# The start of an SSD-and-pooling decoder step on one core: another order of loads, weight splits and adaLN blocks

## The chip, the core and the metric

The kernel runs on one core of a Trainium2 chip. Its engines are PE (matrix products into PSUM), DVE (elementwise), ACT (functions and scaled copies), POOL (elementwise, slower) and SP, which here only issues transfers. Each engine works through its own queue in order; semaphores hold an instruction back until what it needs is there. The metric is the device time in microseconds (us), the median over executions.

## What is computed

A decoder trunk of two layers, on a prompt of 1024 positions and eight short sequences of eight positions (64), so 1088 columns in all. Each layer normalizes x, modulates it by an adaLN vector made from the conditioning c, mixes it and adds it back:

```python
sc = jax.nn.silu(c.astype(jnp.float32))
for i in range(DEPTH):
    mod = sc @ ada_w[i] + ada_b[i]
    shift, scale, gate = jnp.split(mod, 3, axis=-1)
    hn = rmsnorm(x, norm_g[i]) * (1.0 + scale[:, None]) + shift[:, None]
    if i % N_MIXERS == 0:
        out, cv, st = ssd_branch(hn, ...)      # starts with  zxbcdt = h @ w_in
    else:
        out, ps = pool_branch(hn, ...)
    x = x + (1.0 + gate[:, None]) * out
y = rmsnorm(x, final_norm_g)
```

Only the first lines of layer 0 matter here: the sum of squares of x, the adaLN shift and scale, hn, and the first products with w_in.

## The kernel before

x lies transposed: eight tiles of 128 features by 1088 columns (`xs[0..7]`). All 1088 columns are cut into three pieces for PSUM, `CH`, of 368, 368 and 352. To keep fp32 accuracy a matrix is split into a rounded part and the rest (for a weight `hi` on ACT by a copy, `lo` by a subtraction; for activations the tiles named hh and hl), and one product is three matmuls: hi by hh, hi by hl, lo by hh (`mm1`, L190 to L192).

`setup` issues the first loads, computes silu(c) into `scp`, and lets PE run 62 filler products (`warm`). `front` is the stage of this case:

- the squares of the eight x tiles on ACT (L1391, L1395), summed on DVE into `rst` (L1396), the last tile in the three pieces of CH;
- for each piece a matmul with ones that sums over the partitions (L302), logarithm and exponential on ACT (L305, L318), which leave 1/rms in `rst`;
- the adaLN blocks `ada_first(kt)`, kt from 0 to 7, one for each x tile: two halves of 512 KB from `adaA`, eight small matmuls (L261) into the PSUM tile am, a copy on ACT into mp (L266), two selecting matmuls with a 9-column part of the constants kc (L270, "sel" in what follows), and two DVE instructions that leave shift and scale (L280, L281);
- product steps k from 0 to 7. Step k modulates x tile k (`modulate`, L325 to L342: DVE, then ACT for hh, DVE for hl) and multiplies it by slice k of the first two weights, 18 matmuls of 3 pieces each into six PSUM tiles (named mm and p), and then by the small weight wdt (tile pdt, L1431). Step 0 is modulated in three pieces, the others whole.

The first two weights are split whole (`stream_split`, L141 and L145). After step 7 come products with whole streamed weights (tiles wh and wl).

The kernel is written with a tile framework that orders instructions by its own plan; `issue_after(ins)` makes what is inside come behind an instruction in that plan. So the order that counts is that of the built queues.

Of the kernel before, what the change touches and what calls it, by code (L numbers as in the profile page):

```python
# [8 lines left out]
F32 = mybir.dt.float32  # L9
# [35 lines left out]
LAST_USE = {4: 0, 7: 1}  # L45
NSLOT_A = 30
NSLOT_B = 7
NSLOT_E = 4
# [51 lines left out]
class Build:  # L100
# [87 lines left out]
    def mm1(self, ps, w, k, act, ch, first, last):  # L188
        nc, (hi, lo), (ah, al), (a, n) = self.nc, w, act, ch
        nc.tensor.matmul(ps[:, :n], hi[:, k, :], ah[:, a:a + n], start=first, stop=False)  # L190
        nc.tensor.matmul(ps[:, :n], hi[:, k, :], al[:, a:a + n], start=False, stop=False)  # L191
        nc.tensor.matmul(ps[:, :n], lo[:, k, :], ah[:, a:a + n], start=False, stop=last)  # L192

# [8 lines left out]
    def setup(self):  # L202
        nc, io, cp = self.nc, self.io, self.cp
        ct = self.tp.tile([P, 8, 9], F32, tag="ct", name="ct")
        nc.sync.dma_start(ct, io["cT"])
        self.xs = []
        for k in range(8):
            t = self.slots.get("x")
            nc.sync.dma_start(t, io["xT"][k])
            self.xs.append(t)  # L210
        self.vec = cp.tile([P, V_N], F32, tag="vec", name="vec")
        nc.sync.dma_start(self.vec, io["vec"])
        self.kc = cp.tile([P, K_N], F32, tag="kc", name="kc")
        nc.sync.dma_start(self.kc, io["kc"])
        self.ident = self.kc[:, K_ID:K_ID + 128]
# [30 lines left out]


    def ada_block(self, src):

        nc = self.nc  # L250
        raws = []
        for hh in range(2):
            if src is None:
                raws.append(self.stream_next_raw().rearrange("p a m -> p (a m)"))
            else:
# [10 lines left out]
        nc.scalar.activation(mp, pm[:, :256], AF.Copy)  # L266
        yield
        p2 = pm[:, 256:]
        for i in range(2):
            ins = nc.tensor.matmul(p2[:, 16 * i:16 * i + 9], mp[:, 128 * i:128 * i + 128], self.kc[:, K_SEL9:K_SEL9 + 9], start=True, stop=True)  # L270
        self.sel = ins.ins
        yield p2
# [47 lines left out]
    def modulate(self, l, k, x, rst, hi, lo, a, n, t):  # L320
# [13 lines left out]
        if pn < n:  # L334
# [5 lines left out]
            eng.tensor_tensor(out=ts, in0=ts, in1=self.shf[l][:, k, 0:8].unsqueeze(2).to_broadcast([P, 8, 8]), op=ALU.add)  # L340
            nc.scalar.activation(hi[:, s], t[:, pn:n], AF.Copy)
            last = eng.tensor_tensor(out=lo[:, s], in0=t[:, pn:n], in1=hi[:, s].bitcast(F32), op=ALU.subtract)  # L342
# [1039 lines left out]
    def front(self):  # L1382

        nc, io, sl = self.nc, self.io, self.slots
        xs = self.xs
        wdts = sl.get("wdt")
        wdt = wdts[:, :256].rearrange("p (k m) -> p k m", k=8)
        nc.sync.dma_start(wdt, io["wdt"])
        rst = sl.get("rst")
        with self.ln_set():  # L1390
            nc.scalar.activation(rst, xs[0], AF.Square)  # L1391
            for k in range(1, 8):
                sq = self.raw_tile()
                for a, n in CH if k == 7 else ((0, TOK),):
                    nc.scalar.activation(sq[:, a:a + n], xs[k][:, a:a + n], AF.Square)  # L1395
                    nc.vector.tensor_tensor(out=rst[:, a:a + n], in0=rst[:, a:a + n], in1=sq[:, a:a + n], op=ALU.add)  # L1396
# [6 lines left out]
        self.wslots = []  # L1403
# [4 lines left out]
        ws = [self.wsplit.pop(i) for i in range(2)]  # L1408
        self.wpos = 2
        pst = [[self.mm_tile() for _ in range(3)],  # L1410
               [self.pp.tile([P, 512], F32, tag=t, bufs=b, name=self.name("p0")) for t, b in (("y", 2), ("y", 2), ("S", 1))]]
# [513 lines left out]
```

## Time and profile before

| | |
|---|---|
| median of three runs | 1596.21 us (1596.17 to 1596.92) |
| the profiled execution | 1598.18 us |
| its span, first to last instruction | 1596.4 us |
| granted clock of TensorE over the span | 0.997 |
| first product of step 0 | 24.20 us after the span's start |
| first product with a wh tile, behind the eight steps | 67.39 us |

Timeline rows read: start and length in us, engine, line, operation, tile written and tiles read, shapes, number of instructions merged into the row, and in brackets the idle time ahead of it and what ended it. Matmul ends are modelled, so starts are the safer numbers. In the rows a weight load (PEld) is separate from the product (PE).

### The profile page before, as it was taken

Reading aid. Unit: us, or ns where it says so; the run is one execution under the profiler, and the core shown is the slowest. Engines: PE = TensorE matmul, PEld = TensorE weight load, DVE = VectorE, ACT = ScalarE, POOL = GpSimd, SP = SyncE. Lnnn points to the kernel's source line nnn. Section 1 sums busy time; section 2 is a strip of 40 time slices with the busy share of each in tenths; the row PEclk is TensorE's granted clock in tenths of the full one; section 3 lists DMA queues with packets and bytes.
Section 4 is the critical chain, followed back from the end, with each engine's and each line's share of the span. In section 5 each row is a group of like instructions: output and inputs, shape, how many; then the busy total and the mean of one; then the engine's idle time right before and its main releaser. Section 6 shows DMA issues by size and latency. Waiting matters only on the chain.

```text
span 1596.4 us, 30712 instructions
## 1 busy us (share of the span) xinstructions
PE 1573.5 (99%) x11946; PEld 1506.6 (94%) x11946; DVE 1299.4 (81%) x2152; ACT 790.1 (49%) x1512; POOL 519.4 (33%) x558
## 2 busy tenths in 40 slices
PE   8999999999999999999999999999999999999997
PEld 7899999998898998989998999999999999999997
DVE  6874879787888988899888868998889777667886
ACT  6663344466666666674555437533332233233364
POOL 0133556512322413141111232375666630000241
PEclk9999999999999999999999999999999999999999
DMA  9423232355555554679899532233333279566783
GB/s 354 166 101 107 73 112 83 107 185 168 174 161 168 177 195 131 228 245 317 300 336 315 190 128 73 70 133 102 116 113 110 104 246 371 137 180 178 164 170 118
DMA packets 122306, 275.59 MB, mean 173 GB/s; under 512 B 18192, under 2 KB 59312, under 8 KB 122160
## 3 DMA queue, kind: packets, MB, share of 16 engines
q1 hardware_dynamic: 118128, 260.90, 48.0%
q0 software_dynamic: 4032, 12.72, 4.7%
q8 instruction: 94, 1.54, 0.4%
q14 instruction: 52, 0.43, 0.1%
HBM read 201.12 MB, written 70.23 MB: 170 GB/s over the span
## 4 chain that ended last, share of the span: by engine, by line
PE 79%; DVE 8%; issue 4%; DMA 4%; ACT 4%; POOL 1%; SPq 0%; DVEq 0%; ACTq 0%; POOLq 0%
PE st L1061 10%; PE st L1059 10%; PE st L1060 10%; PE mm L190 10%; PE mm L191 9%; PE mm L192 9%; PE op L1278 2%; PE op L1279 2%; PE op L1277 2%; DMA acb<-acd 2%; PE S L616 2%; PE y L638 2%; DVE raw L368 1%; PE tr L577 1%; DVE xbc L359 1%
## 5 line engine op out<-in xcount | busy, mean ns | idle before, releaser
L1059 PE MATMUL st<-hh,w 128*128 128x272 f32 x832 | 240.5, 289 | 0.9 <-ACT w L182 0.9
L1061 PE MATMUL st<-hh,w 128*128 128x272 f32 x832 | 240.7, 289 | 0.4 <-DVE w L184 0.4
L1060 PE MATMUL st<-hl,w 128*128 128x272 f32 x832 | 240.3, 289 | 0.0
L1059 PE MATMUL st<-t,w 128*128 128x272 f32 x624 | 179.8, 288 | 0.0
L1061 PE MATMUL st<-t,w 128*128 128x272 f32 x624 | 179.7, 288 | 0.0
L1060 PE MATMUL st<-t,w 128*128 128x272 f32 x624 | 179.4, 287 | 0.0
L190 PE MATMUL mm<-hh,wh 128*128 128x368 f32 (+1 forms) x528 | 178.3, 338 | 0.0
L191 PE MATMUL mm<-hl,wh 128*128 128x368 f32 (+1 forms) x528 | 174.7, 331 | 0.0
L192 PE MATMUL mm<-hh,wl 128*128 128x368 f32 (+1 forms) x528 | 173.2, 328 | 0.0
L1059 PEld LDWEIGHTS st<-hh,w 128*128 128x128 f32 x832 | 156.9, 189 | 1.3 <-ACT w L182 1.3
L1061 PEld LDWEIGHTS st<-hh,w 128*128 128x128 f32 x832 | 156.6, 188 | 0.9 <-DVE w L184 0.9
L1060 PEld LDWEIGHTS st<-hl,w 128*128 128x128 f32 x832 | 156.9, 189 | 0.0
L182 ACT ACTIVATE w<-wr 128x512 fp32r<-128x512 f32 x104 | 64.9, 629 | 166.4 <-PE st L1061 137.4
L624 POOL TENSOR_TENSOR hd<-h,cd 128x256 f32<-128x256 f32 x56 | 47.2, 842 | 293.5 <-DVE h L625 146.5
L1278 PE MATMUL op<-b,w 128*128 128x272 f32 x448 | 129.2, 288 | 0.7 <-DVE b L1207 0.7
L1277 PE MATMUL op<-b,w 128*128 128x272 f32 x448 | 129.6, 289 | 0.0
L1279 PE MATMUL op<-b,w 128*128 128x272 f32 x448 | 129.1, 288 | 0.0
L190 PE MATMUL mm<-gh,wh 128*128 128x368 f32 (+1 forms) x372 | 125.6, 339 | 0.0
L192 PE MATMUL mm<-gh,wl 128*128 128x368 f32 (+1 forms) x372 | 122.2, 328 | 0.0
L191 PE MATMUL mm<-gl,wh 128*128 128x368 f32 (+1 forms) x372 | 122.0, 328 | 0.2 <-DVE gl L791 0.2
L1059 PEld LDWEIGHTS st<-t,w 128*128 128x128 f32 x624 | 117.8, 189 | 0.1
L1061 PEld LDWEIGHTS st<-t,w 128*128 128x128 f32 x624 | 117.5, 188 | 0.0
(310 smaller groups left out, 4593.8 us busy)
## 6 DMA issues: line engine op xcount, KB each, us to landing
wr<-win SPq DMA_DIRECT2D x48, 512.0 KB, 3.6
wr<-pin SPq DMA_DIRECT2D x32, 512.0 KB, 3.6
acb<-acd SPq DMA_DIRECT2D x62, 256.0 KB, 4.1
wr<-pout SPq DMA_DIRECT2D x28, 512.0 KB, 5.0
x<-x1d SPq DMA_DIRECT2D x24, 544.0 KB, 6.7
x1d<-x SPq DMA_DIRECT2D x22, 544.0 KB, 4.6
wr<-pout POOLq DMA_DIRECT2D x20, 512.0 KB, 5.7
x<-xT SPq DMA_DIRECT2D x16, 544.0 KB, 6.6
```

The lines of the kernel that those rows point to most:

```text
L182: self.nc.scalar.activation(hi, src, AF.Copy)
L190: nc.tensor.matmul(ps[:, :n], hi[:, k, :], ah[:, a:a + n], start=first, stop=False)
L191: nc.tensor.matmul(ps[:, :n], hi[:, k, :], al[:, a:a + n], start=False, stop=False)
L192: nc.tensor.matmul(ps[:, :n], lo[:, k, :], ah[:, a:a + n], start=False, stop=last)
L616: nc.tensor.matmul(S[:, 256 * i:256 * i + 256], Bt, xde.rearrange("p r q -> p (r q)"), start=True, stop=True)
L624: nc.gpsimd.tensor_tensor(out=hd, in0=h[-1], in1=cd.unsqueeze(2).to_broadcast([P, 4, 64]), op=ALU.mult)
L1059: nc.tensor.matmul(ps[c][:, :QUART], hi[:, k], xh[:, t], start=(k == 0), stop=False)
L1060: nc.tensor.matmul(ps[c][:, :QUART], hi[:, k], xl[:, t], start=False, stop=False)
L1061: nc.tensor.matmul(ps[c][:, :QUART], lo[:, k], xh[:, t], start=False, stop=(k == 3))
L1277: nc.tensor.matmul(ps[:, :QUART], hi[:, k], xh, start=k == 0, stop=False)
L1278: nc.tensor.matmul(ps[:, :QUART], hi[:, k], xl, start=False, stop=False)
L1279: nc.tensor.matmul(ps[:, :QUART], lo[:, k], xh, start=False, stop=k == 7)
```

## The change

Five things are different.

1. **Loads.** vec, the nine sel columns of kc (with one more), the first two of eight slices of the first two weights (`WK`), and the first half of adaLN block 0 go ahead of the x tiles. The second half of block 0 and the other six slices of both weights follow x. wdt and the rest of kc are issued from inside step 0.
2. **Splits.** The two weights are split in two parts each: slices 0 and 1 early (ACT and POOL), slices 2 to 7 behind the modulation of steps 0 and 1 (ACT and DVE).
3. **Squares.** The last two x tiles are squared and added by pieces, not the last alone.
4. **Block 0** is computed among the sums over the partitions instead of behind them.
5. **Blocks 1 to 3** have fixed places: behind the products (k, weight, piece) of `FIRST`; blocks 4 to 7 behind the last product of the steps before.

Slots of the same size are used as before, and nothing behind the front is edited. The diff, cut to its core:

```diff
+WK = 2
+FIRST = {(0, 0, 1): 1, (1, 0, 0): 2, (1, 1, 2): 3}
...
-        nc.tensor.matmul(ps[:, :n], lo[:, k, :], ah[:, a:a + n], start=False, stop=last)
+        return nc.tensor.matmul(ps[:, :n], lo[:, k, :], ah[:, a:a + n], start=False, stop=last)
...
-        self.xs = []
-        for k in range(8):
-            t = self.slots.get("x")
-            nc.sync.dma_start(t, io["xT"][k])
-            self.xs.append(t)
         self.vec = cp.tile([P, V_N], F32, tag="vec", name="vec")
         nc.sync.dma_start(self.vec, io["vec"])
         self.kc = cp.tile([P, K_N], F32, tag="kc", name="kc")
-        nc.sync.dma_start(self.kc, io["kc"])
+        nc.sync.dma_start(self.kc[:, K_SEL9:K_SEL64], io["kc"][:, K_SEL9:K_SEL64])
+        raws = [self.wp.tile([P, 8, P], F32, tag="wr", bufs=3, name=self.name("wr")) for _ in range(2)]
+        for i, t in enumerate(raws):
+            nc.sync.dma_start(t[:, :WK], self.items[i][0][:, :WK])
+        self.ada0 = [self.slots.get("ada") for _ in range(2)]
+        self.xs = [self.slots.get("x") for _ in range(8)]
+        self.load_ada(self.ada0[0], 0, 0)
+        for k in range(8):
+            nc.sync.dma_start(self.xs[k], io["xT"][k])
+        self.load_ada(self.ada0[1], 0, 1)
+        for i, t in enumerate(raws):
+            nc.sync.dma_start(t[:, WK:], self.items[i][0][:, WK:])
+        self.firsts = [self.split_first(t) for t in raws]
...
+        def part(a, b, eng):
+            self.nc.scalar.activation(hi[:, a:b], raw[:, a:b], AF.Copy)
+            eng.tensor_tensor(out=lo[:, a:b], in0=raw[:, a:b], in1=hi[:, a:b].bitcast(F32), op=ALU.subtract)
...
-        wdts = sl.get("wdt")
-        wdt = wdts[:, :256].rearrange("p (k m) -> p k m", k=8)
-        nc.sync.dma_start(wdt, io["wdt"])
         rst = sl.get("rst")
+        for _, _, part in self.firsts:
+            part(0, WK, nc.gpsimd)
...
-                for a, n in CH if k == 7 else ((0, TOK),):
+                for a, n in CH if k > 5 else ((0, TOK),):
...
+            self.ada_first(0)
             for a, n in CH:
                 self.ms_log(rst, rst, a, n, 1.0 / 1024, "mm", 3)
                 self.rstd(rst[:, a:a + n])
-        self.ada_first(0)
...
-        lower = [self.stream_split(i, True) for i in range(2)]
         with self.tc.issue_after(self.sel):
             self.warm(8, "mm", 3)
-        self.ada_first(1)
...
+        lower = [functools.partial(f[2], WK, 8, nc.vector) for f in self.firsts]
...
         for k in range(8):
-            if k < 6:
-                self.ada_first(k + 2)
+            if 1 < k < 6:
+                with self.tc.issue_after(mm.ins):
+                    self.ada_first(k + 2)
...
-                if lower:
+            if lower:
+                with self.tc.issue_after(last.ins), self.tc.issue_after(self.mod_hi.ins):
                     lower.pop(0)()
...
-                    self.mm1(pst[i][c], ws[i], k, (hi, lo), CH[c], k == 0, k == 7)
+                    mm = self.mm1(pst[i][c], ws[i], k, (hi, lo), CH[c], k == 0, k == 7)
+                    if (k, i, c) in FIRST:
+                        with self.tc.issue_after(mm.ins):
+                            self.ada_first(FIRST[k, i, c])
+                if k + i == 0:
+                    nc.sync.dma_start(wdt, io["wdt"])
+                    for a, b in ((0, K_SEL9), (K_SEL64, K_N)):
+                        nc.sync.dma_start(self.kc[:, a:b], io["kc"][:, a:b])
```

The built queues show where this puts things. SP's queue at the start of the program, before, from the last x tile on (the seven others and ct stand ahead; ada_324 and ada_326 are block 0, ada_362 begins block 1):

```order
L209 DMA x_191<-xT 128x1088
L212 DMA vec<-vec 128x282
L214 DMA kc<-kc 128x778
L1388 DMA wdt_282<-wdt 128x256
L257 DMA ada_324<-adaA 128x1024
L257 DMA ada_326<-adaA 128x1024
L121 DMA wr_343<-win 128x1024
L121 DMA wr_348<-win 128x1024
L257 DMA ada_362<-adaA 128x1024
```

The same queue now, from its first transfer to the first x tile (wr_181 and wr_182 are the two weights, ada_185 the first half of block 0):

```order
L207 DMA ct<-cT 128x72
L209 DMA vec<-vec 128x282
L211 DMA kc<-kc 128x10
L214 DMA wr_181<-win 128x256
L214 DMA wr_182<-win 128x256
L269 DMA ada_185<-adaA 128x1024
L219 DMA x_187<-xT 128x1088
```

So five transfers moved ahead of x; behind the eight x tiles stand ada_186, the two remaining weight parts (128x768), both halves of block 1, then wdt and kc.

PE's queue between the 62 fillers and the first product (mm_381), before; ms_320 is the third and last of the sums over the partitions:

```order
L302 MATMUL ms_320<-rst_284,ones 128x352
L261 MATMUL am_328<-ada_324,scp 32x256 x4
L261 MATMUL am_328<-ada_326,scp 32x256 x4
L270 MATMUL am_328<-kc,mp_337 128x9 x2
L245 MATMUL warm_353<-ones 128x128 x8
L190 MATMUL mm_381<-hh_407,w_13_345 128x368
```

The same place now, with all three sums (ms_347, ms_351, ms_355):

```order
L286 MATMUL am_332<-ada_185,scp 32x256 x4
L327 MATMUL ms_347<-rst_296,ones 128x368
L286 MATMUL am_332<-ada_186,scp 32x256 x4
L327 MATMUL ms_351<-rst_296,ones 128x368
L295 MATMUL am_332<-kc,mp_341 128x9 x2
L327 MATMUL ms_355<-rst_296,ones 128x352
L254 MATMUL warm_359<-ones 128x128 x8
L192 MATMUL mm_369<-hh_376,w_11_207 128x368
```

Block 0 moved in among the sums, and the third sum now stands between sel and the eight fillers.

ACT's queue from the end of block 0 to hh of step 1, before (hh_407 is step 0's, hh_469 step 1's; mp_375 belongs to block 1, w_13 and w_15 are the two weights):

```order
L266 ACTIVATE mp_337<-am_328 128x256
L141 ACTIVATE w_13_345<-wr_343 128x1024
L331 ACTIVATE hh_407<-x_177,shf_274 128x368 x2
L141 ACTIVATE w_15_350<-wr_348 128x1024
L333 ACTIVATE x_177<-x_177,shf_274 128x368 x2
L331 ACTIVATE hh_407<-x_177,shf_274 128x288
L341 ACTIVATE hh_407<-x_177 128x64
L266 ACTIVATE mp_375<-am_366 128x256
L333 ACTIVATE x_177<-x_177,shf_274 128x288
L331 ACTIVATE hh_469<-x_179,shf_274 128x1024
```

And now, from the second piece of step 0 on (hh_376 is step 0's, hh_441 step 1's, mp_416 belongs to block 1):

```order
L356 ACTIVATE hh_376<-x_187,shf_288 128x368
L358 ACTIVATE x_187<-x_187,shf_288 128x368
L356 ACTIVATE hh_376<-x_187,shf_288 128x288
L358 ACTIVATE x_187<-x_187,shf_288 128x368
L358 ACTIVATE x_187<-x_187,shf_288 128x288
L366 ACTIVATE hh_376<-x_187 128x64
L263 ACTIVATE w_11_207<-wr_181 128x768
L291 ACTIVATE mp_416<-am_407 128x256
L356 ACTIVATE hh_441<-x_188,shf_288 128x1024
```

The weight split moved behind all pieces of step 0, ahead of block 1's copy; the second weight's now stands behind hh of step 1. On PE block 1 stands whole between products of step 0, with 17 of its 18 products ahead of its sel; blocks 2, 4 and 7 stand between products of steps 1, 2 and 5, and blocks 3, 5 and 6 next to pdt. Before, blocks 1 and 2 were worked ahead of step 1's products, block 3 between products of step 1, and blocks 4 to 7 behind pdt. Behind step 7 the queues hold the same instructions, some DVE, ACT and SP rows up to the second pair of products in another order.

More of the change, by code (lines that the diff above doesn't have):

```diff
@@ L245, in warm, with split_first, load_ada @@
             self.nc.tensor.matmul(ps[:, :128], self.ones, self.ones, start=True, stop=True)
+    def split_first(self, raw):
+        hl = [self.slots.get("w0", F32R) for _ in range(2)]
+        hi, lo = (t[:, :1024].rearrange("p (k m) -> p k m", k=8) for t in hl)
+        def part(a, b, eng):
+            self.nc.scalar.activation(hi[:, a:b], raw[:, a:b], AF.Copy)
+            eng.tensor_tensor(out=lo[:, a:b], in0=raw[:, a:b], in1=hi[:, a:b].bitcast(F32), op=ALU.subtract)
+        return hl, (hi, lo), part
+    def load_ada(self, t, kt, hh):
+        self.nc.sync.dma_start(t[:, :1024].rearrange("p (a b) -> p a b", a=4), self.io["adaA"][0, kt][:, 4 * hh:4 * hh + 4, :])
     def ada_block(self, src):
@@ L1399, in front @@
                 self.rstd(rst[:, a:a + n])
[L1400 removed]
         self.hn = []
[L1403 to L1404 removed]
         with self.tc.issue_after(self.sel):
             self.warm(8, "mm", 3)
[L1407 to L1408 removed]
         self.wpos = 2
+        wdts = sl.get("wdt")
+        wdt = wdts[:, :256].rearrange("p (k m) -> p k m", k=8)
+        ws = [f[1] for f in self.firsts]
+        self.wslots = [t for f in self.firsts for t in f[0]]
+        lower = [functools.partial(f[2], WK, 8, nc.vector) for f in self.firsts]
         pst = [[self.mm_tile() for _ in range(3)],
```

4 lines of the change are left out of this document (3 added, 1 removed).

## The prediction

> **What bounds the kernel now.** I read the page first, then the busy time by stretches, then the timeline of the first 68 us engine by engine, because the diff touches nothing later than that.
>
> ```profile
> span 1596.4 us, 30712 instructions
> PE 1573.5 (99%) x11946; PEld 1506.6 (94%) x11946; DVE 1299.4 (81%) x2152; ACT 790.1 (49%) x1512; POOL 519.4 (33%) x558
> 24.20:33.04 8.84, 7.71 (x63) 4.36 (x62) 6.65 (x15) 5.22 (x10) 0.00 (x0) 1.00 1.01 405
> 67.39:116.00 48.61, 48.61 (x343) 48.61 (x343) 40.25 (x70) 32.57 (x56) 10.90 (x10) 1.00 0.27 99
> ```
>
> The columns of the last two rows are stretch, length, then busy time of PE, weight load, DVE, ACT and POOL, granted clock, DMA share, GB/s. PE is the bound of the whole; behind 67.39 it is full, so whatever the front wins or loses there goes through to the end. Only before 33.04 does PE stand and wait. What it waits for is the chain from the last x tile to the first product:
>
> ```profile
> 6.69 1.11 ACT L1395 ACTIVATE raw<-x 128x1088 f32<-128x1088 f32 x1 [0.26 <-DMA x<-xT]
> 14.90 1.30 ACT L1395 ACTIVATE raw<-x 128x368 f32<-128x368 f32 x3 [0.26 <-DMA x<-xT]
> 16.69 0.24 DVE L231 TENSOR_SCALAR cwh<-vec 128x160 f32<-128x160 f32 x1 [0.58 <-DMA vec<-vec]
> 16.95 1.42 DVE L1396 TENSOR_TENSOR rst<-rst,raw 128x368 f32<-128x368 f32 x3
> 17.54 2.10 PE L302 MATMUL ms<-rst,ones 128*128 128x368 f32 x6 [0.94 <-DVE rst L1396]
> 18.46 0.57 ACT L305 ACTIVATE rst<-ms,eps 128x368 f32<-128x368 f32 x1 [1.56 <-PE ms L302]
> 19.06 0.51 ACT L318 ACTIVATE rst<-rst 128x368 f32<-128x368 f32 x1
> 19.48 0.99 ACT L305 ACTIVATE rst<-ms,eps 128x368 f32<-128x368 f32 x2
> 21.28 1.17 DVE L338 TENSOR_TENSOR x<-x,rst 128x64 f32<-128x64 f32 x8 [2.56 <-ACT rst L318]
> 21.30 0.38 ACT L266 ACTIVATE mp<-am 128x256 f32<-128x256 f32 x1
> 21.73 0.61 PE L270 MATMUL am<-kc,mp 128*128 128x9 f32 x4 [0.50 <-ACT mp L266]
> 22.20 2.03 PE L245 MATMUL warm<-ones 128*128 128x128 f32 x16
> 22.45 0.23 DVE L280 TENSOR_SCALAR shf<-am,vec 128x9 f32<-128x9 f32 x1
> 22.91 1.11 DVE L325 SCALAR_TENSOR_TENSOR x<-x,scl,rst 128x368 f32<-128x368 f32 x2
> 23.55 1.12 ACT L331 ACTIVATE hh<-x,shf 128x368 fp32r<-128x368 f32 x2 [0.64 <-DVE x L325]
> 24.20 0.95 PE L190 MATMUL mm<-hh,w 128*128 128x368 f32 x2
> ```
>
> The last x tile is squared from 14.90; the additions of its pieces wait on DVE behind two instructions that need vec; all three pieces go through logarithm and exponential before adaLN block 0 is copied (21.30); the first product starts at 24.20. Next is the way to product step 1:
>
> ```profile
> 23.94 1.22 DVE L145 TENSOR_TENSOR w<-wr,w 128x1024 fp32r<-128x1024 f32 x1
> 24.57 1.04 ACT L141 ACTIVATE w<-wr 128x1024 fp32r<-128x1024 f32 x1
> 30.52 1.28 DVE L325 SCALAR_TENSOR_TENSOR x<-x,scl,rst 128x1024 f32<-128x1024 f32 x1
> 31.84 1.15 ACT L331 ACTIVATE hh<-x,shf 128x1024 fp32r<-128x1024 f32 x1 [2.13 <-DVE x L325]
> 33.04 0.60 PE L190 MATMUL mm<-hh,w 128*128 128x368 f32 x2 [0.48 <-ACT hh L331]
> ```
>
> The weight splits (1.04 and 1.22 us each, two of each) stand among step 0's pieces on ACT and DVE, and step 1 starts at 33.04.
>
> **The change, part by part.** First the loads. SP's transfers, and the landing of x:
>
> ```profile
> x<-xT SPq DMA_DIRECT2D x8, 544.0 KB, 8.2
> ada<-adaA SPq DMA_DIRECT2D x15, 512.0 KB, 10.3
> vec<-vec SPq DMA_DIRECT2D x1, 141.0 KB, 11.2
> 1.50:2.00 0.50, 0.50 (x4) 0.50 (x4) 0.00 (x0) 0.50 (x1) 0.00 (x0) 1.00 0.25 46
> 5.00:5.50 0.50, 0.50 (x7) 0.50 (x7) 0.00 (x0) 0.18 (x1) 0.00 (x0) 1.00 1.04 409
> ```
>
> From 6.69 to 14.90 six x tiles land, 1.37 us for 544 KB, or 397 KB a microsecond. Now vec (141), one half block (512), a quarter of two weights of the half block's size (2 x 128) and 5 KB of kc go ahead: 914 KB, 2.30 us, so the last x would land at 17.20. The first half microseconds move little (46 GB/s against 409 later), which small loads can fill: 0.44 us of such a window. Bounds: 14.9 if all were hidden; 18.6 if a loss that lies behind x today came ahead of it (vec is waited for until 16.69, 1.79 us after x, though 141 KB take 0.36: 1.4 us lost). I take **16.8**, nearest to the rate of the x rows.
>
> [...]
>
> Squares and sums: a third of 1.30 for the first piece (17.23), a third of 1.42 for its addition (17.75, as vec is long there; x6's pieces were added before), 0.12 to PE as between 17.42 and 17.54: 17.87. First logarithm 0.92 later (17.54 to 18.46), exponential 0.60 later, then mp 0.42 later (19.06 to 19.48) since ACT now has it third: 19.8, against 21.30. The block's second half lands 1.3 us behind x and is covered by the logarithm. sel 0.43 later (21.30 to 21.73): 20.24. Then stands the third sum's matmul, 0.47 for sel and a third of 2.10, and the eight warm products, 2.0: first product **23.4**, 0.8 earlier. The modulation would be there by 20.24 + 0.72 + 0.46 + 0.64 + 0.65 = 22.7 (the steps 21.73, 22.45, 22.91, 23.55, 24.20), so the filler holds PE; were it no cover, 0.7 more. The eight L338 (1.17) leave this path: two go behind the pieces, six behind the last one.
>
> The small weight parts: two POOL and two ACT operations at about 5 us, on engines that wait for x; nothing if the parts land before x0, at most 1 us of ACT, caught up by the 0.26 waits per tile. The remaining three quarters of the splits (0.8 and 0.9 us each) follow step 0's and step 1's pieces. wdt and the rest of kc go behind block 1: some 22.9, needed about 28; block 1 itself about 22.6, needed at 25.2. The narrowest cover is these 2.6 us.
>
> Then PE's own work, from these rows:
>
> ```profile
> 34.92 0.33 PE L191 MATMUL mm<-hl,w 128*128 128x368 f32 x1
> 36.18 0.44 PE L192 MATMUL mm<-hh,w 128*128 128x368 f32 x1
> 45.91 0.51 PE L270 MATMUL am<-kc,mp 128*128 128x9 f32 x4
> 46.27 0.41 PE L191 MATMUL mm<-hl,w 128*128 128x368 f32 x1
> 48.73 0.75 PE L1431 MATMUL pdt<-x,wdt 128*32 128x256 f32 x8
> 50.27 0.44 PE L190 MATMUL mm<-hh,w 128*128 128x368 f32 x1
> 59.04 0.74 PE L1431 MATMUL pdt<-x,wdt 128*32 128x256 f32 x8
> 59.71 0.44 PE L190 MATMUL mm<-hh,w 128*128 128x368 f32 x1
> 63.55 0.44 PE L190 MATMUL mm<-hh,w 128*128 128x368 f32 x1
> 67.39 0.44 PE L190 MATMUL mm<-hh,wh 128*128 128x368 f32 x1
> ```
>
> A step without a block is 3.84 (59.71 to 63.55), of it pdt 0.67, so a product is 0.176. A block behind pdt adds 0.87 (48.73 to 50.27 less 0.67). A block between products takes 1.26 in place of 0.17 (34.92 to 36.18), and the product behind it 0.44 instead of 0.33: 1.21. sel adds 0.36 and the same tail: 0.44.
>
> Step 0 now: 17 products (2.99) and block 1 between them (1.21) stand ahead of block 1's sel: 27.6. From sel to step 1's first product 0.72 + 0.46 + 1.32 + 1.20 (the last from 30.52, 31.84, 33.04): **31.3**, 1.74 earlier. mp for it stands on ACT behind the pieces and 0.8 of weight split, about 27.0, so hidden by 0.6.
>
> Behind it, today: seven steps 26.88, six sels 2.64, four blocks behind pdt 3.48, one between products 1.21, in all 34.21; the trace has 34.35 (33.04 to 67.39), so 0.14 of waits. Changed: block 2 comes only now, and blocks 2, 4 and 7 stand between products: 26.88 + 2.64 + 3 x 0.87 + 3 x 1.21 = 35.76. New waits (step 1's hl, step 2's hh) are unknown; bounds nothing and 0.5, I take today's 0.14. End of the steps: 31.3 + 35.90 = 67.2, against 67.39: **0.2 us earlier**. What is won ahead of step 1 is paid back by a block that no longer fills that wait. The profiled execution took 1598.18 (span 1596.4 and 1.8 around it), 2.0 above the median of the three runs, 1596.21; the difference is taken off the median: 1596.0.
>
> **The rivals.** *The wait fills* (faster): PE stands 2.4 us ahead of step 1 in my sum (27.6 + 0.44 + 0.18 + 0.67 = 28.9 to 31.3). If the operands come sooner and nothing else waits, the steps end at 23.4 + 30.72 + 7 x 0.44 + 4 x 1.21 + 3 x 0.87 = 64.65: 2.7 us gained, 1593.5. For it: ACT and DVE are lighter by the splits; against: sel to product is a chain of four fixed steps, 3.7 us.
>
> *x comes late* (slower): the 1.4 us that are lost today behind x fall ahead of it. Everything behind x shifts by that, 1596.0 + 1.4 = 1597.4; it decides from a last x later than 17.0, where my gain is used up. For it: the loss is in the trace, and x's end now lies in its time.
>
> *PE slows down in the gap*: at the start the fillers run 4 in half a microsecond at 1.5 us and 7 at 5.0, though the granted clock reads 1.00 in both. If the 2.4 us wait ahead of step 1 brings that rate back for 3 us, 3 x 3/7 = 1.3 us are lost: 1597.3. Against it: after today's wait of 0.94 at 17.54 the two matmuls of a sum take no longer than the next ones, so the chance is small.
>
> [...]
>
> **How the numbers follow.** Forecast 0.5 (own range 1595.0 to 1597.0), the wait fills 0.28, x late 0.14, PE slow 0.08. 0.2%, about what a measurement of this kernel can tell from no change, is 3.2 us. More than that is gained only where the wait fills and x is early too: a third of that rival, 0.09. More is lost only where late x, new waits and slowness meet: 0.04. The range takes in most of the filled case and the late one: 1593.8 to 1597.8.
>
> **What would show it.** The first square of the last x tile at 16.8; mp of block 0 ahead of the second logarithm at 19.8; the first product at 23.4 right behind the fillers; step 1's first at 31.3 with ACT hh as releaser; the first product with wh (now 67.39) at 67.2. Last x beyond 17.5, a wait at block 1 for its load, or steps 2 to 7 longer than 36.2 us in sum make it wrong to the slow side; a wait ahead of step 1 below 1 us to the fast one.

## The result, and the profile after

| | before | changed |
|---|---|---|
| median of six runs | 1596.57 us (1595.46 to 1601.27) | 1605.43 us (1604.20 to 1610.08) |
| profiled execution, span | 1598.18, 1596.4 | 1604.20, 1602.4 |
| first product of step 0 | 24.20 | 28.84 |
| first product of step 1 | 33.04 | 36.53 |
| first product with wh | 67.39 | 75.86 |

The changed kernel is slower: ratio 1.0059, 95% interval 1.0046 to 1.0071. The forecast was 1596.0, from 1593.8 to 1597.8; it was wrong by 9.4 us. The profile of the changed kernel is that of its fastest run; up to the first wh product it shows 8.47 us more than before, which is about what the medians show (8.86). Behind the first wh product the eighteen profiled executions of this document's kernels take 1525.8 to 1529.7 us with no order by kernel, so a single execution scatters by some 4 us there, and the experiments are read by the starts inside the front.

The head of the page of the changed kernel (span, busy time, share and instructions of each engine): the busy times are those of before to within 3 us.

```profile
span 1602.4 us, 30718 instructions
PE 1574.1 (98%) x11946; PEld 1506.1 (94%) x11946; DVE 1299.0 (81%) x2154; ACT 791.0 (49%) x1516; POOL 522.0 (33%) x560
```

So the loss is waiting, and slow work, in the front. Rows of ACT's timeline of the changed kernel, from the first x tile to the first logarithm (the last row of squares holds three pieces each of the seventh and eighth tile):

```profile
9.99 1.11 ACT L1415 ACTIVATE rst<-x 128x1088 f32<-128x1088 f32 x1 [1.97 <-DMA x<-xT]
17.66 1.11 ACT L1419 ACTIVATE raw<-x 128x1088 f32<-128x1088 f32 x1 [1.14 <-DMA x<-xT]
19.01 2.66 ACT L1419 ACTIVATE raw<-x 128x368 f32<-128x368 f32 x6 [0.24 <-DMA x<-xT]
24.05 0.57 ACT L330 ACTIVATE rst<-ms,eps 128x368 f32<-128x368 f32 x1 [2.39 <-PE ms L327]
```

The first square comes at 9.99, before it was 5.32; the eighth tile from about 19.01 + 1.33 = 20.34, before from 14.90. One tile on the way (17.66) is late by another 0.9. Then PE:

```profile
22.42 1.59 PE L327 MATMUL ms<-rst,ones 128*128 128x368 f32 x2 [4.65 <-DVE rst L1420]
26.09 0.51 PE L295 MATMUL am<-kc,mp 128*128 128x9 f32 x4
27.13 1.95 PE L254 MATMUL warm<-ones 128*128 128x128 f32 x16
28.84 0.41 PE L192 MATMUL mm<-hh,w 128*128 128x368 f32 x1
36.53 1.27 PE L192 MATMUL mm<-hh,w 128*128 128x368 f32 x3 [2.15 <-ACT hh L356]
44.63 0.60 PE L192 MATMUL mm<-hh,w 128*128 128x368 f32 x2 [0.31 <-ACT hh L356]
69.18 0.43 PE L193 MATMUL mm<-hl,w 128*128 128x368 f32 x1 [1.35 <-DVE hl L357]
```

The first sum, two instructions, takes 1.59 us; before, the six of all three sums took 2.10. The three products at 36.53 take 1.27; without the slow clock three take 0.76 (e7 below). The windows of the same kernel say why (columns as in the prediction; the third from the right is the granted clock, the last two DMA share and GB/s):

```profile
4.50:5.00 0.50, 0.50 (x4) 0.50 (x4) 0.00 (x0) 0.38 (x1) 0.05 (x1) 1.00 0.61 160
8.50:9.00 0.50, 0.50 (x6) 0.50 (x6) 0.00 (x0) 0.00 (x0) 0.00 (x0) 1.00 1.03 418
22.50:25.84 3.34, 3.34 (x12) 1.23 (x13) 0.75 (x2) 1.39 (x3) 0.00 (x0) 0.50 1.04 398
36.08:39.49 3.41, 2.96 (x12) 2.52 (x16) 2.29 (x3) 2.43 (x4) 0.00 (x0) 0.50 0.05 17
```

The clock is 0.50 for 3.4 us twice, once from the end of the wait of 4.65 and once from within that of 2.15. And at 4.5 us the loads move 160 GB/s, where the kernel before had reached 400:

```profile
4.50:5.00 0.50, 0.50 (x7) 0.50 (x6) 0.00 (x0) 0.00 (x0) 0.00 (x0) 1.00 0.99 400
```

Three suspects, then: the loads ahead of x, the clock, and the new places of blocks and instructions. The experiments take them apart. Each ratio is to the kernel before on the same chip; starts are from each run's profile.

### The profile page after: what moved, and what is told of

Its sections match the earlier page's. It is cut to its first block, busy times and chain, and to the rows that moved or that the text cites. A ratio compares the mean times of both kernels' runs of the same rounds, so it can differ in the third digit from the quotient of the medians.

```text
span 1602.4 us, 30718 instructions
## 1 busy us (share of the span) xinstructions
PE 1574.1 (98%) x11946; PEld 1506.1 (94%) x11946; DVE 1299.0 (81%) x2154; ACT 791.0 (49%) x1516; POOL 522.0 (33%) x560
```

## Experiments on the loads

**e1: x first.** The order of the loads is undone. Two things follow it: the early weight copies stand behind the squares, as they would otherwise wait ahead of them, and the plan puts block 0 behind the sums again.

```diff
+        for k in range(8):
+            nc.sync.dma_start(self.xs[k], io["xT"][k])
         self.vec = cp.tile([P, V_N], F32, tag="vec", name="vec")
...
-        for k in range(8):
-            nc.sync.dma_start(self.xs[k], io["xT"][k])
+        self.load_ada(self.ada0[0], 0, 0)
         self.load_ada(self.ada0[1], 0, 1)
```

> The changed kernel with one thing undone: the eight x tiles are the first loads behind ct again, and vec, the sel columns, the small weight parts and the first half of block 0 follow them; the early weight copies on ACT stand behind the squares, so that they do not wait ahead of them, and the plan puts block 0 behind the sums again. Loads theory (the transfers ahead of x cost far more than their size): the first piece of the last x tile is squared at 14.9 again (20.3 in the changed kernel, 14.90 before), the first product comes at 22.5 to 24.2 (28.84), TensorE waits less than 2 us ahead of the sums and its clock stays at 1.00 there, the first wh product at 67 to 69 (75.86), the time at 1595 to 1599. Rival (the block places and the splits cost it): the first product is early, but steps 1 to 7 still take 39.3 us in sum, and the time stays above 1600. Rival (another run of the same state of the chip would have had x early): x is late here too.

First square 5.28, first product 23.85, first wh product 69.94; ratio 1.0028 (1.0017 to 1.0039). Up to the first wh product 5.92 of the 8.47 us are back, 4.99 of them at the first product: the loads, with the idle time and the slow sums that follow from them, are the larger part of the loss. But steps 1 to 7 still take 37.93 us, and the time is not back: both the first theory and its rival hold a part.

**e2, e3, e5, e6, e13, e14: which load.** e1 with these lines put ahead of the x tiles (e3 has those of e6 and e14, e5 those of e2 and its own, e13 those of e2 and its own, where the other weight follows whole behind x; where the weight parts come early, in e3 and e14, their copies are ahead of the squares again):

```diff
 # e2
+        self.load_ada(self.ada0[0], 0, 0)
 # e5
+        self.load_ada(self.ada0[1], 0, 1)
 # e6
+        nc.sync.dma_start(self.vec, io["vec"])
+        nc.sync.dma_start(self.kc[:, K_SEL9:K_SEL64], io["kc"][:, K_SEL9:K_SEL64])
 # e13
+        nc.sync.dma_start(raws[0], self.items[0][0])
 # e14
+        for i, t in enumerate(raws):
+            nc.sync.dma_start(t[:, :WK], self.items[i][0][:, :WK])
```

> The changed kernel with vec, the sel columns and the small weight parts (402 KB in rows of 40 to 1128 bytes) behind x; only the half block of adaLN (512 KB) is ahead of it; the early weight copies stand behind the squares. If the small rows are what crawls: the half block costs its size, 512 KB at 397 KB/us = 1.3 us, so the last x tile is squared from 16.2 to 16.7, first product 24 to 25.5, time 1596 to 1599. If whatever goes first crawls (the start of the queue is slow for all): last x at 17.5 to 19, time 1599 to 1603. If the half block itself is the cause: last x at about 19, time near 1603.

> The changed kernel with the first half of adaLN block 0 behind x; vec, the sel columns and the small weight parts stay ahead. If the small rows are the cause: last x tile at 18 to 19 (3 to 4 us late for 1.0 us worth of bytes), first product above 26, time 1601 to 1604. If the half block is the cause: last x at 15.9 to 16.3, time 1596 to 1598.

> Both halves of adaLN block 0 (1024 KB) ahead of x, all small loads behind it; otherwise as the kernel with one half ahead, whose first square came at 7.58, 2.26 us after the 5.32 of before, for 1.29 us worth of bytes. If a new array pays once when it is first read (the half block's 0.97 us beyond its size): first square at 7.58 + 1.29 = 8.9. If every transfer ahead pays: 5.3 + 2 x 2.26 = 9.8. If it is the start of the queue that is slow whatever it carries: at 8.9 too, and the GB/s of the half microseconds are those of the one-half kernel.

> Only vec and the sel columns (146 KB in rows of 1128 and 40 bytes, 0.37 us by size) ahead of x, the small weight parts behind it. With the weight parts ahead as well (402 KB) the first square came at 8.05, 2.73 us late. If the loss goes with the bytes of small rows: 5.3 + 2.73 x 146/402 = 6.3. If each new array pays a fixed loss, 0.37 + 2 x 0.6 to 2 x 1.0: 6.9 to 7.7. If the weight parts alone are slow: 5.7.

> Two arrays ahead of x, both in rows of 4096 bytes and of 512 KB each: the first half of adaLN block 0 and one whole weight; all else behind x. Both halves of block 0 ahead (one array, as many bytes) gave the first square at 8.39, 0.5 us beyond their size. If every new array that is read first pays 0.5 to 1 us: first square at 8.9 to 9.4. If only the small rows (40 to 1128 bytes) pay: 8.3 to 8.6.

> Only the two small weight parts (256 KB in rows of 1024 bytes, 0.65 us by size) ahead of x. If the small rows pay: first square at 6.7 to 7.1 (from 5.3), as the step from vec alone (6.44) to vec and parts (8.05) was 1.6 us. If a new array pays once: 6.5 to 7.0 too, and then the run with a whole weight and a half block must have paid twice. If neither: 5.95.

| ahead of x | KB | by size, at 397 KB/us | first square | later than 5.32 | beyond its size |
|---|---|---|---|---|---|
| nothing (eight kernels) | 0 | 0 | 5.00 to 5.65 | | |
| e6: vec, sel columns | 146 | 0.37 | 6.44 | 1.12 | 0.75 |
| e14: weight parts | 256 | 0.64 | 7.33 | 2.01 | 1.37 |
| e3: vec, sel, weight parts | 402 | 1.01 | 8.05 | 2.73 | 1.72 |
| e2: half a block | 512 | 1.29 | 7.58 | 2.26 | 0.97 |
| e5: a whole block | 1024 | 2.58 | 8.39 | 3.07 | 0.49 |
| e13: half a block, a whole weight | 1024 | 2.58 | 8.47 | 3.15 | 0.57 |
| the change (and e4, e10, e16) | 914 | 2.30 | 9.99 (10.50 to 10.59) | 4.67 to 5.27 | 2.4 to 3.0 |

The table goes by the first square, not by the last tile that the expectations name, because in e2 and e3 the last tile's squares wait for DVE (0.98 and 0.55 us), not for a load. The eight kernels with nothing ahead spread over 0.65 us, and each other row is one trace, so only differences well above that count. Large rows cost half a microsecond to one beyond their size, little more than the scatter, and no more from two arrays than from one (e5 against e13: "each new array pays" falls). The small loads cost 1.7 us beyond theirs, with 402 of the 914 KB. Added to the 0.97 of the half block that makes 2.7, inside the 2.4 to 3.0 of the change. Two expectations were missed altogether: e5 came earlier than its 8.9 and 9.8, e14 later than its 6.7 to 7.1. e3's window shows that this isn't a queue that stands still: the DMA engines are 0.98 busy and move 107 GB/s.

```profile
4.50:5.00 0.50, 0.50 (x4) 0.50 (x4) 0.00 (x0) 0.37 (x1) 0.05 (x1) 1.00 0.98 107
```

Why the small loads take so long there isn't settled. Whole times: e2 1.0023 (1.0011 to 1.0035), e3 1.0048 (1.0033 to 1.0063); one run each of e5 (1600.37), e6 (1600.80), e13 (1605.02) and e14 (1600.90 us). The first square isn't the whole loss: e13 has it where e5 has, but also one late tile (16.66, after a wait of 1.64) and a wait of 1.01 at step 6, and its first wh product comes at 75.32 against 72.51.

## Experiments on the clock

**e4: fillers in both gaps** of the changed kernel. `fill(tile, n, column, width)` issues n products of ones by ones of that width; the tile is that of the 62 fillers, and then block 1's, in columns that nothing else uses.

```diff
         self.wps = self.warm(62)
+        self.fill(self.wps, 24, 0, 8)
...
+            if k == 0:
+                with self.tc.issue_after(mm.ins):
+                    self.fill(self.am, 8, 384, 128)
```

> The changed kernel with fillers in TensorE's two gaps and no other instruction moved: 24 products of 128x8 behind the 62 fillers (estimate 0.18 us each from the sel rows, 4.3 us of the 4.65 us wait) and 8 of 128x128 behind the pdt products of step 0 (2.0 us of the 2.15 us wait). Clock theory (a wait of TensorE halves its clock for about 3.4 us): the granted clock reads 1.00 from 22 to 26 and from 36 to 39.5, the first product comes 1 to 1.9 us earlier (27 to 27.8 in place of 28.84), the way from step 1's first product to step 2's shrinks from 8.10 to about 6.6, the time goes down by 2.4 to 3.4 us to about 1602.5. If the second gap alone holds the clock (the 128x8 fillers may count as too little work): half of it. Rival (the clock is no cause; ACT and DVE set these stages): the stages keep their lengths, the time stays at 1605 or grows.

PE's timeline and windows of e4, at the first gap and at the second:

```profile
15.74 6.88 PE L259 MATMUL warm<-ones 128*128 128x128 f32 x61
35.21 2.05 PE L259 MATMUL am<-ones 128*128 128x128 f32 x16
37.42 0.77 PE L192 MATMUL mm<-hh,w 128*128 128x368 f32 x3 [0.17 <-ACT hh L361]
```

```profile
22.75:26.15 3.40, 3.12 (x18) 0.70 (x10) 1.84 (x5) 0.99 (x3) 0.00 (x0) 0.50 0.99 365
36.00:39.50 3.50, 3.28 (x24) 2.48 (x26) 2.65 (x6) 2.81 (x4) 0.00 (x0) 1.00 0.33 131
```

The second gap behaves as the clock theory says: 1.00, three products in 0.77, and 7.13 us from step 1 to step 2 in place of 8.10. The first doesn't: with PE's row full up to 22.6 by fillers of 128x8 the clock fell all the same. x came later still (first square 10.59), and the time, 1.0049 (1.0034 to 1.0064), can't be told from the change's; its first wh product is at 75.63.

**e10: the same with 22 fillers of 128x128** in the first gap.

```diff
-        self.fill(self.wps, 24, 0, 8)
+        self.fill(self.wps, 22, 0, 128)
```

> The changed kernel with 22 more fillers of 128x128 behind the 62 (5.5 us) and 8 ahead of step 1; the plan then also moves the first sums and the copy of block 0 by one place each. The 24 fillers of 128x8 had kept TensorE's queue busy and the clock had fallen to 0.50 all the same. If the clock goes by the work in the array and not by whether the queue is busy: 1.00 throughout here, the way from the first sum to the first product falls from 6.42 to 5.3 to 5.9. If the fall has another cause: 0.50 here too.

```profile
22.51 0.89 PE L332 MATMUL ms<-rst,ones 128*128 128x368 f32 x2
26.97 0.44 PE L192 MATMUL mm<-hh,w 128*128 128x368 f32 x1
```

No window below 1.00 anywhere in the front; from first sum to first product 4.46 us (6.42 in the change). Some of the 1.96 is the plan's other order: all of block 0's eight first products now stand ahead of the first sum. From the last tile's first square to the first product, which doesn't depend on that, it is 6.90 in place of 8.50. The first wh product comes at 73.20, 2.66 earlier than in the change, though the first square is 0.57 later. One run, 1604.61 us.

**e7: x first, and the second gap filled.** Nothing else moves against e1.

```diff
+            if k == 0:
+                with self.tc.issue_after(mm.ins):
+                    self.fill(self.am, 8, 384, 128)
```

> The kernel with x first again, and 8 fillers of 128x128 between step 0's pdt products and step 1's first product; no other instruction moves. Clock theory: in the kernel without them TensorE waits 1.99 us ahead of step 1 (32.01) and the granted clock is 0.50 from 32.0 to 35.3; with them it stays at 1.00, the way from step 1's first product to step 2's goes from 8.67 to 7.0 to 7.3, and the first wh product comes about 1.5 us earlier (from 69.94 to 68.4): time 1 to 1.6 us less. Rival (step 1's length is set by ACT and DVE): unchanged within 0.3 us, and the wait only moves into step 1 and ahead of step 2.

The rows of e1, then of e7, at step 1:

```profile
32.01 1.27 PE L192 MATMUL mm<-hh,w 128*128 128x368 f32 x3 [1.99 <-ACT hh L356]
```

```profile
30.43 2.05 PE L258 MATMUL am<-ones 128*128 128x128 f32 x16
32.49 0.76 PE L192 MATMUL mm<-hh,w 128*128 128x368 f32 x3
40.02 0.60 PE L192 MATMUL mm<-hh,w 128*128 128x368 f32 x2 [0.70 <-ACT hh L360]
```

Step 1 takes 7.53 us (7.0 to 7.3 expected), not 8.67: 1.14 less, with the clock at 1.00. The step's start is 0.48 later in e7 (its sums were), so the first wh product comes at 69.27, 0.67 earlier. Ratio 1.0011 (0.9998 to 1.0023), from 1.0028. A wait of 1.99 us had cost more than a microsecond behind itself.

**e9: the kernel before, made to wait.** 53 fillers for 62.

```diff
-        self.warm(62)
+        self.warm(53)
```

> The kernel before with 53 fillers at the start in place of 62; no other instruction moves. TensorE then waits some 3.2 us ahead of the first sum (0.94 + 9 x 0.25) in place of 0.94, while x, DVE and ACT are as before. Clock theory: the granted clock falls to 0.50 for about 3.4 us around the sums, the sums start at 17.5 as before, but the first product comes 0.5 to 1.5 us later than 24.20 and the first wh product as much later than 67.39; time 0.5 to 1.5 us more. This is the price of the cold sums in the changed kernel. Rival (ACT's chain of logarithm and exponential hides slow sums): clock low, first product within 0.2 us of 24.20.

```profile
17.19 3.31 PE L302 MATMUL ms<-rst,ones 128*128 128x368 f32 x6 [2.51 <-DVE rst L1396]
24.90 0.95 PE L190 MATMUL mm<-hh,w 128*128 128x368 f32 x2
```

```profile
17.95:21.35 3.40, 3.40 (x17) 1.42 (x19) 0.40 (x3) 2.46 (x5) 0.00 (x0) 0.50 1.02 418
```

The sums take 3.31 in place of 2.10, and from the first sum to the first product it is 7.71 in place of 6.66: cold sums cost about 1.05 us. The first wh product is 0.70 later (68.09). In the whole time that is not seen: 0.9999 (0.9990 to 1.0008), an interval wider than 0.70 us.

## Experiments on places and neighbours

**e8: x first, the fixed block places undone.**

```diff
-            if 1 < k < 6:
-                with self.tc.issue_after(mm.ins):
-                    self.ada_first(k + 2)
+            if k < 6:
+                self.ada_first(k + 2)
```

> The kernel with x first, and the fixed places of adaLN blocks 1 to 7 undone: each block is asked for where the kernel before did, two steps ahead, and the plan sets it. Order theory (block 2 no longer fills the wait ahead of step 1, and stands later between products): block 2 goes back into step 0's end, TensorE's wait ahead of step 1 shrinks to 1.2 us or less and the clock stays at 1.00; from step 1's first product to the first wh product it takes 34.3 to 35.5 us (37.93 with the fixed places, 34.35 before), the first wh product comes at 66.5 to 68, the time at 1595 to 1598. Rival (the places cost nothing; splits and the clock do): that way stays at 37 us or more, time as with x first alone.

The wait ahead of step 1 is 1.13 us and the clock stays at 1.00. From step 1 to the first wh product it takes 36.26 us, not the 34.3 to 35.5 expected (37.93 in e1, 36.78 in e7); ratio 1.0008 (0.9995 to 1.0021). Of the 1.67 us between e1 and e8, 1.15 go already in e7, with the places kept, so it may look as if the places cost only half a microsecond. But e8 loses time in step 7, which takes 4.77 us where e1 and e7 take 3.83:

```profile
65.58 0.43 PE L193 MATMUL mm<-hl,w 128*128 128x368 f32 x1 [0.64 <-DVE hl L357]
60.70 2.32 DVE L350 SCALAR_TENSOR_TENSOR x<-x,scl,rst 128x1024 f32<-128x1024 f32 x1
```

A DVE instruction of 1.28 takes 2.32 there beside two additions on POOL (58.41 to 61.95); e16 below tries such a pair. Steps 1 to 6 alone take 34.10 us in e1, 32.95 in e7, 31.49 in e8 and 30.51 in the kernel before: 1.15 for the clock and, with the clock at 1.00 in both, 1.46 for the places. The expected 34.3 to 35.5 would have been met without the loss in step 7 (35.3). What keeps the other 1 us was not tried.

**e11: only the squares by pieces**, in the kernel before.

```diff
-                for a, n in CH if k == 7 else ((0, TOK),):
+                for a, n in CH if k > 5 else ((0, TOK),):
```

> The kernel before with the squares and additions of the last two x tiles by pieces instead of the last alone. My step took the pieces of the seventh tile as added before the last lands. If so: sums at 17.3 to 17.6 (17.54). If DVE is full there (its three additions of 1088 columns end 1.47 us after the last square of the seventh tile): three additions for one cost 0.3 to 0.5 us, but the wait for vec at 16.69 hides it: sums at 17.5 to 17.8. In both cases the time is within its scatter of the kernel before.

First sum at 17.28, one run of 1596.43 us: no price. (Its first product came at 25.24, since the clock was 0.50 from 22.75 to 26.15 in this run, behind short waits alone.) In the changed kernel, where vec no longer holds DVE up, its timeline shows what does (the first row holds one whole tile and three pieces):

```profile
18.80 2.83 DVE L1420 TENSOR_TENSOR rst<-rst,raw 128x1088 f32<-128x1088 f32 x4 [0.84 <-ACT raw L1419]
21.64 0.33 DVE L485 MEMSET raw<- 128x320 f32 x1
21.89 1.36 DVE L1420 TENSOR_TENSOR rst<-rst,raw 128x368 f32<-128x368 f32 x3
```

DVE adds without a break until 21.6, then runs a memset, and takes the last tile's first piece at 21.89, some 1.1 us after its square (20.34 and a third of 1.33).

**e16: POOL later.** Behind step 4 the changed kernel loses time that no clock explains. DVE and POOL of the changed kernel there:

```profile
63.16 1.28 POOL L1049 TENSOR_TENSOR sw<-wr 128x512 f32<-128x512 f32 x1 [55.86 <-DMA wr<-win]
64.53 1.29 POOL L1050 TENSOR_TENSOR sw<-sw,wr 128x512 f32<-128x512 f32 x1
65.77 2.27 POOL L1054 TENSOR_TENSOR wr<-wr,wr 128x512 f32<-128x512 f32 x1
64.60 2.29 DVE L350 SCALAR_TENSOR_TENSOR x<-x,scl,rst 128x1024 f32<-128x1024 f32 x1
66.82 2.30 DVE L357 SCALAR_TENSOR_TENSOR hl<-x,shf,hh 128x1024 fp32r<-128x1024 f32 x1
```

Two DVE instructions of 1.28 take 2.3 beside POOL's additions, and PE waits 1.35 for the second (69.18 above). The kernel before has such a pair too, but there no product waits for it:

```profile
57.63 2.32 DVE L325 SCALAR_TENSOR_TENSOR x<-x,scl,rst 128x1024 f32<-128x1024 f32 x1
```

In e16 the first addition waits for the last hl of the steps:

```diff
+            if self.hold:
+                self.tc.add_manual_dep(ins.ins, self.hold.name, mybir.DependencyInfo(mybir.DependencyClass.Sync, mybir.DependencyReason.DATA), reason="hold")
```

> The changed kernel with one wait added: the first of the three additions on POOL that begin the weight sums (63.16 to 68.04 in the changed kernel) waits for the last hl of the eight steps; the order of all queues is unchanged. In the changed kernel two DVE instructions that lie beside them took 2.29 and 2.30 us in place of 1.28, and TensorE waited 1.35 us for the second (step 6, 69.18). Sharing theory (DVE and POOL slow each other down): no DVE instruction of the steps takes over 1.4 us, the wait at step 6 falls below 0.4, the two steps 5 and 6 shrink by 1.0 to 1.5 us together. If the additions are now late for the products that use them, that time is lost again behind the steps: the first wh product is early by 1 to 1.5 us relative to step 4, the time the same within 1 us. Rival (the wait at step 6 comes from DVE's order alone, POOL has no part): DVE's two instructions still take 2.3, or the wait stays above 1 us.

```profile
74.23 1.71 POOL L1049 TENSOR_TENSOR sw<-wr 128x512 f32<-128x512 f32 x1 [67.81 <-DVE hl L367]
68.75 1.28 DVE L350 SCALAR_TENSOR_TENSOR x<-x,scl,rst 128x1024 f32<-128x1024 f32 x1
71.28 1.28 DVE L357 SCALAR_TENSOR_TENSOR hl<-x,shf,hh 128x1024 fp32r<-128x1024 f32 x1
```

Step 6 takes 3.84 us in place of 5.46, its wait is gone, and steps 2 to 5 take what they took (6.96, 5.16, 3.67 and 6.14 us): POOL was the cause. Behind the first wh product e16 takes 1529.7 us, at the upper end of the scatter, so what the late additions cost there can't be told. Nor does the time tell, 1.0070 (1.0043 to 1.0096), because in the profiled run the clock stayed low for far longer:

```profile
21.50:31.75 10.25, 9.52 (x35) 6.63 (x36) 5.34 (x15) 5.79 (x12) 0.00 (x0) 0.50 1.04 408
```

**e12 and e15: an attempt at a better kernel**, from the kernel before: x first, block 0 directly behind it, the instructions that need vec behind the additions; e15 also keeps the first weight copy ahead of step 0.

```diff
+            with self.tc.issue_after(self.add):
+                nc.vector.tensor_scalar(self.cwh, self.vec[:, V_CW:V_CW + 160], 0.5, None, op0=ALU.mult)
+                nc.vector.tensor_scalar(self.adab1, self.vec[:, V_ADAB:V_ADAB + 48], 1.0, None, op0=ALU.add)
...
+                with self.tc.issue_after(self.wcopy[0]):
+                    last = self.modulate(0, k, xs[k], rst, hi, lo, a, n, xs[k][:, a:a + n])
```

> From what the runs point to: the kernel before, with x first, block 0's two halves directly behind x and vec, kc and wdt behind them, and the two instructions that need vec (and a memset) behind the additions of the last x tile on DVE. No fillers, splits or block places are touched. DVE adds the last pieces from 16.1, not 16.95: first sum at 16.6 (17.54), first product at 23.2 to 23.5 (24.20), steps as before (8.84 and 34.35), first wh product at 66.4 to 66.8, time 0.5 to 1 us less than the kernel before. If the loads behind (weights, block 1) now bound step 0: nothing gained. If TensorE's earlier end of the steps is lost later: first wh product early, time the same.

> The run with block 0's load directly behind x had the sel products 0.8 us early, but the plan had put both whole weight copies on ACT behind step 0's first pieces, and the first product waited 1.44 us for one. Here the first weight copy is ordered ahead of them, as in the kernel before; nothing else is edited. First product at 23.3 to 23.7 (24.20 before, 24.85 without the order), first wh product at 66.4 to 67.0, time 0.4 to 1 us below the kernel before. If the copy now waits for its load (0.17 us before) or DVE's subtraction is late: first product at 24 to 24.5 and no gain.

One row of e12, then one of e15:

```profile
24.85 0.44 PE L190 MATMUL mm<-hh,w 128*128 128x368 f32 x1 [1.44 <-ACT w L141]
```

```profile
26.32 0.44 PE L191 MATMUL mm<-hl,w 128*128 128x368 f32 x1 [1.74 <-DVE hl L336]
```

Sel came 0.82 earlier in e12 (20.91 for 21.73), and the plan handed it back to a weight copy; with the copy in place the first product was at 23.62, as expected, and two products later PE waited for DVE. First wh product at 68.16 and 68.32, ratios 1.0013 (1.0003 to 1.0023) and 1.0012 (1.0000 to 1.0024): no gain. No kernel here beat the one before.

## Why the prediction was wrong

| term | forecast | measured | what the runs show |
|---|---|---|---|
| squares of the last x tile from | 16.8 | 20.3 | loads ahead of x: e1, e2, e3 |
| from there to the first sum | 1.07 | 2.1 | DVE still adds the seventh tile (rows below; e12) |
| first sum to first product | 5.53 | 6.42 | half clock: e9 (in the kernel before), e10 |
| first product to step 1 | 7.9 | 7.69 | as forecast |
| step 1 to the first wh product | 35.90 | 39.33 | half clock 0.97 (e4), POOL 1.62 (e16), 0.84 left |
| first wh product | 67.2 | 75.86 | |

**The step that failed first is "I take 16.8, nearest to the rate of the x rows."** The last tile was squared from 20.3. The rival "x comes late" named the mechanism; its size, 1.4 us, was too small. The rate of 397 KB a microsecond belongs to rows of 4352 bytes in full flow. The loads that were put ahead were partly small and ran at the very start: 914 KB cost 4.7 us at the first x tile where I had 2.30 less 0.44. Both corrections to the 2.30 that I weighed were read wrongly from the kernel before. The 0.44 took the slow first half microseconds for room that small loads can fill, but already in the second of them the DMA engines are 0.96 busy; and the 1.4 took the wait for vec for a loss, but while vec is waited for the loads run at 371 GB/s, so it came late beside the bytes of other transfers:

```profile
2.00:2.50 0.50, 0.50 (x4) 0.50 (x3) 0.00 (x0) 0.03 (x1) 0.00 (x0) 1.00 0.96 141
15.00:15.50 0.50, 0.50 (x7) 0.50 (x6) 0.50 (x1) 0.50 (x2) 0.00 (x0) 1.00 1.01 371
```

So no row priced small loads at the start; e3, e6 and e14 do. The late tile at 17.66 came on top. It doesn't follow from the order of the loads alone: with the same order e4 has a tile 1.6 us late, e10 and e16 have none. Its cause was not tried.

**The second is the rival "PE slows down in the gap", set aside by a wait of 0.94.** One short wait can't show what a longer one does. The wait ahead of step 1 was forecast at 2.4 and was 2.15, the loss was put at 1.3 and was 0.97; the 3 us of slow work in that sum, an estimate, were 3.41 at a clock of 0.50 (36.08 to 39.49 above). So a slower PE behind the wait and its price were right, the chance of 0.08 was not. And I didn't apply it to the other wait: x late by some 2 us, with the fillers and block 0's first products done by 17.8, already meant an idle PE ahead of the sums.

**The third is "x6's pieces were added before".** The sum took DVE to be free when the last tile's first piece is squared. In the kernel before it adds whole tiles until 16.11, 1.21 us after the last tile's squares begin, so taking vec out of its way could not bring the first sum to 1.07 us:

```profile
7.83 8.28 DVE L1396 TENSOR_TENSOR rst<-rst,raw 128x1088 f32<-128x1088 f32 x6 [4.50 <-ACT raw L1395]
```

The pieces make little difference: e12, with the seventh tile whole and both vec and the memset behind, needs 1.94 us, the change 2.08, the kernel before 2.64. (The sum itself has 17.75 where its terms add up to 17.70; nothing hangs on it.)

**What was right:** block 0 among the sums and the way from the first product to step 1 (7.69), and that blocks 2, 4 and 7 alone between products pay the early step 1 back: with the clock and POOL taken out (39.33 - 0.97 - 1.62 = 36.74) my 35.90 is short by 0.84. Most of that lies in step 1: by the forecast's terms it is 3.84 + 1.21 + 0.44 + 0.87 = 6.36, and with the clock held it takes 7.13 (e4). The wait at step 2 (44.63) is 0.31 of it; the rest stays open.

**The chances:** I treated late x, new waits and a slow PE as rivals and gave their meeting 0.04. They weren't independent: the late x made PE wait 4.65 us, and at the end of that wait the clock fell to 0.50. POOL's additions were no rival in the forecast at all. Beside them DVE takes 2.32 for 1.28 in the kernel before too (57.63), where they begin with step 5 (55.25); in the change they begin 2.7 us into it (63.16) and catch two instructions on DVE, the second of which step 6 waits for.

## What to carry to other kernels

Before you put transfers ahead of the one that everybody waits for, price them by the GB/s of the stretch where they will run and by their row size, not by the rate of the large transfers: here 402 KB in rows of 40 to 1128 bytes took 1.72 us beyond their size (e3), 512 to 1024 KB in rows of 4096 bytes 0.49 to 0.97 (e2, e5, e13). Count another microsecond behind a wait of TensorE of about 2 us: at waits of 2.15 (the change) and 1.99 us (e1) the clock fell to 0.50 for 3.4 us, and with eight fillers of 128x128 in the wait it stayed at 1.00 and the step behind it was 0.97 (e4) and 1.14 us (e7) shorter; a wait of 2.66 us in e14 left it at 1.00. And when a stage moves or is put in another order, look up what other engines will be doing beside it, here POOL, beside whose additions a DVE instruction of 1.28 us took 2.3.

## What the runs showed of the hardware that was not expected

- **With how little idleness the clock fell to 0.50.** It did in waits, or within 2 us behind them, of 2.15 (the change), 1.99 (e1) and 1.8 us (e2, e3, e5, e6, e14) ahead of step 1, not with 1.13 (e8). But length alone doesn't decide: ahead of the sums of e14 a wait of 2.66 us left the clock at 1.00, and so did waits of 1.74 (e15) and 1.68 (e2), while in e11 it fell behind waits of 0.65 and less.

```profile
19.24 1.50 PE L327 MATMUL ms<-rst,ones 128*128 128x368 f32 x4 [2.66 <-DVE rst L1420]
```

The two stretches in the changed kernel start at 22.4 and 36.1 (the clock is 0.92 from 22.0 to 22.5 and 0.58 from 36.0 to 36.5), 13.7 us apart, four times their length of 3.4. What decides besides a wait's length was not tried.

- **How long it lasts.** A stretch took 3.4 us in most runs, but 10.25 in e16, with PE busy for 9.52 of it, and 6.8 later in the same run (38.6 to 45.4). The six runs of the changed kernel, from 1604.20 to 1610.08 us, have mean clocks from 0.997 to 0.993. The two slowest have 0.993 and 0.994, but 1605.09 has 0.994 as well. 0.003 of 1600 us is 4.8 us, so the clock alone could make most of that spread; that it does is not shown.
- **Which fillers held the clock.** 24 fillers of 128x8 filled PE's row up to 22.6 and did not hold the clock (e4, 0.50 from 22.75); 22 of 128x128 did (e10, 1.00). Each is one profile.
- **DVE and POOL.** In the change two DVE instructions of the steps (L350 and L357, 128x1024) took 2.29 and 2.30 us beside POOL's additions, 1.28 elsewhere, and the third of those additions (128x512) took 2.27, the two before it 1.28 and 1.29. They end one after the other, at 65.82 (POOL), 66.89 (DVE), 68.04 (POOL) and 69.12 (DVE), as if they took turns. Why they slow each other down is not shown.
